# A two-layer hybrid decoder step: streamed operands moved to 16 bytes past 32, the opening splits taken by turns, the shared bias chain given priority, and the retention's old states loaded into two large slots

## The chip, the cores and the metric

The kernel runs on one core of one Trainium2 chip. The metric is device time in microseconds of one execution, lower is better. TensorE is called PE below (PEld is its loading of weights), VectorE DVE, ScalarE ACT, GpSimd POOL and SyncE SP.

## The reference

A step of a two-layer decoder on 256 prompt tokens and 8 decode tokens, all float32. Each layer runs three mixers on the same input, merges them through gates, and ends in two residual norms and a feed-forward block:

```python
u = x @ w_in                       # 1024 -> 8464 columns
q_r, k_r, v_r, g_r, z, xbc, dt_raw, q_c, k_c, v_c, gates = split(u)
o_r, s_ret_new = _retention(rotary(q_r), rotary(k_r) * RET_DK ** -0.5, v_r, s_ret)
br_a = (head_norm(o_r) * silu(g_r)) @ w_br_ret
xs, bm, cm = split(silu(causal_conv(xbc, s_conv)))
y, s_ssm_new = _ssd(xs, softplus(dt_raw + dt_bias), -exp(a_log), bm, cm, s_ssm)
br_b = group_rms((y + d_skip * xs) * silu(z)) @ w_br_ssd
o_c = sliding_window_attention(q_c, k_c, v_c, kbuf, vbuf, sinks, rel_bias)
br_c = o_c @ w_br_swa
g_a, g_b, g_c = split(sigmoid(gates), 3)
x = layer_norm(ALPHA * x + (g_a * br_a + g_b * br_b + g_c * br_c) @ w_out)
x = layer_norm(ALPHA * x + (silu(x @ w_ffn_gate) * (x @ w_ffn_up)) @ w_ffn_down)
```

The decode tokens need old states: `state_ret` (8 sequences x 4 heads x 128 x 128 per layer), `state_ssm`, convolution rows and key/value caches. All new states are outputs.

## The kernel before

**Activations are stored as [128 features, 264 tokens]**: 256 prompt tokens and 8 decode tokens side by side. A weight block of 128x128 is PE's stationary operand and a 264-column activation tile is streamed past it. To keep float32 accuracy from the fast float32r mode, every operand is split into a high and a low part. ACT writes the high part (`wh`, `xh`), DVE subtracts to get the low part (`wl`, `xl`), and `mm3` runs three matmuls per block: `wh` with `xh`, `wh` with `xl`, `wl` with `xh`. A product over 1024 features is a `gemm` of eight blocks k = 0..7, 24 matmuls into one PSUM bank.

**Where the streamed tiles lie.** The layer input is one tile for each part, `x{h,l}` of [128, 8, T + 2] with T = 264, so block k starts k * 1064 bytes behind a tile that starts at a multiple of 32. The blocks k = 0..7 start 0, 8, 16, 24, 0, 8, 16, 24 bytes past a multiple of 32. The other streamed float32r tiles are slots of 8 * T columns (`T8`: `chl`, `rhl`, `yhl`, `mh`, `ml`) or of T columns (`fh`, `fl`, the feed-forward hidden tiles). 264 columns are 1056 bytes, 33 times 32, so all of their blocks start at a multiple of 32.

**The stages of a layer.** `mixers` runs in this order: products for keys and values, queries, retention values, queries and keys, B and C of the state-space mixer (SSD), gates, and its inputs (all appear as `ps_u`); then the branches, each with gate products (`ps_gate`) and a branch product (`ps_br`); then the output product (`ps_o`). `ffn` follows with gate and up products (`ps_fg`, `ps_fu`) and the down product (`ps_fd`). `ps_z` are products on an input that is not normalized yet, with two more columns.

**What runs between.** Attention (`swa`), retention (`ret`), the SSD decay and body (`ssd_decay`, `ssd`) and state updates are generators in a queue; `pump` takes a step of one after each product. A scheduler that simulates the program then sets the final order on every engine, from the order of the code, priorities (`high_priority`) and explicit edges (`issue_after`). Each engine works through its own list in order, so whatever stands at the head of a list and waits holds up what is behind it.

**Names that the change touches.** `load_x` loads and transposes the input (`ps_x`, 24 transposes) and splits it with `xsplit`; before it, 16 matmuls on constants (`ps_warm`) run. `halves` makes the first six products of layer 0 (key/value and queries). `bias_table` builds attention's position bias: `ps_rb`, a row in DRAM, then two tables `bias`. `ret` needs old retention states in `rs0` (shown as `rs`): 512 KB per head, in a pool of two slots `SI`; head h + 1 is asked for when head h is used. 32 matmuls `ps_rso` per layer read them. `ssd` loads its old states into the same two `SI` slots (`s`). `T8` has three slots in turn: attention's result `chl`, its two tables of scores `lg`, later `rhl`, `xdt`, `yhl` and others. `on` (normalized retention output) is transposed into `ps_rt`.

Of the kernel before, what the change touches and what calls it, by code (L numbers as in the profile page):

```python
# [10 lines left out]
F32 = mybir.dt.float32  # L11
F32R = mybir.dt.float32r
AF = mybir.ActivationFunctionType
ALU = mybir.AluOpType
# [6 lines left out]
SEQ = 256  # L21
NS = 8
T = SEQ + NS
KB = D // 128
N_IN = 8464
D_FF = 2816
KF = D_FF // 128
# [5 lines left out]

WARM = 16
CONV = 1536

QR, KR, VR, GR, ZZ, XBC, DT, QC, KC, GATE = 0, 512, 1024, 1536, 2048, 3072, 4608, 4624, 5136, 5392
# [10 lines left out]
def _constants():  # L48

    secs = {}  # L50
# [12 lines left out]
    c0 = (i[None, :] >= p[:, None]).astype(np.float64)  # L63
    secs["mask"] = np.concatenate([c0, c0[:, :128]], 1)
    lg = np.log(1.0 - 2.0 ** (-5.0 - np.arange(4)))
# [41 lines left out]
class Kern:  # L107
# [88 lines left out]
    def wsplit(self, raw, shape, into=None):  # L196

        n = int(np.prod(shape))
        if into is None:
            pool = self.hps[self.nsplit % len(self.hps)]  # L200
            self.nsplit += 1
            into = tuple(pool.tile([128, 1024], F32R, tag=t, bufs=3 if pool is self.hp else 1, name=t) for t in ("wh", "wl"))
        h, l = into
        spec = {2: "p (a b) -> p a b", 3: "p (a b c) -> p a b c"}[len(shape)]
        kw = dict(zip("abc", shape))
        kw.pop("abc"[len(shape) - 1])
        hv, lv = h[:, :n].rearrange(spec, **kw), l[:, :n].rearrange(spec, **kw)
        hf = h[:, :n].bitcast(F32).rearrange(spec, **kw)
        with self.tc.high_priority(200):
            self.act(hv, raw)  # L210
            self.sub(lv, raw, hf)
# [27 lines left out]
    def load_x(self):  # L239
        nc, a, cp = self.nc, self.a, self.cp  # L240
        keep = _OFF["onehot"][0]
        self.cst = cp.tile([128, keep], F32, name="cst")
        nc.sync.dma_start(self.cst[:, 0:256], a["cst"][:, 0:256])

        self.xb = [self.xp.tile([128, KB, T + 2], F32R, name=f"x{c}") for c in "hl"]
        self.xw = [tuple(t[:, k] for t in self.xb) for k in range(KB)]
        self.x = [(h[:, :T], lo[:, :T]) for h, lo in self.xw]
        xt = [self.T4("xt")[:, :D] for _ in range(2)]
        xs = self.T4("xts")[:NS, :D]
        nc.sync.dma_start(xt[0], a["x_prompt"][0, 0:128])  # L250
        nc.sync.dma_start(xt[1], a["x_prompt"][0, 128:256])
        nc.sync.dma_start(xs, a["x_sample"][:, 0])
        self.neg = cp.tile([128, 128], F32R, name="neg")
        nc.vector.memset(self.neg.bitcast(F32), -1.0 / 128)
        self.par = [None] * DEPTH
        ps = self.pg("ps_warm")
# [3 lines left out]
        next(bias)  # L260
        self.queue.append(bias)
        for k in range(KB):
# [55 lines left out]
    def bias_table(self):  # L318
# [10 lines left out]
        self.ld(row[:, 383:385], a["sinks"].rearrange("l h -> h l"))  # L329
        yield  # L330
        ps = self.pm("ps_rb")
        self.mm(ps[:8, :129], rb, oh)
# [5 lines left out]
        for h in range(2):  # L338
            self.ld(self.bias[h], once[4 * h : 4 * h + 4].unsqueeze(1).to_broadcast([4, 128, 383]))
        yield  # L340

# [191 lines left out]
    def T8(self, name, dt=F32):  # L533
        return self.slot("t8", 8 * T, 3, name, dt)

# [24 lines left out]
    def mixers(self, l):  # L560
# [10 lines left out]
        def halves(c0, n, name, pieces, shape):  # L571

            pss = [self.pg("ps_u") for _ in range(n)]
            for i in range(2):
                raw = self.strip([(0, 128, self.win(l, c0, n * 128)[:, 4 * i : 4 * i + 4])], (4, n * 128), name)
                for u in range(0, n, 2):
# [256 lines left out]
    def ssd_decay(self, l, dtf):  # L833
# [35 lines left out]
        ps = self.pm("ps_cs")  # L869
        self.mm(ps[:, 0:32], self.c("mask")[:, :128], da[:, :32])  # L870
        self.mm(ps[:, 32:64], self.c("ones"), da[:, :32])
# [35 lines left out]
    def ssd(self, l):  # L907
# [45 lines left out]
        for g in range(2):  # L953
            ps = self.pm("ps_cb")
            self.mm(ps[:, 0:256], B(g)[:, 0:128], C(g)[:, 0:256])
            self.mm(ps[:, 256:384], B(g)[:, 128:256], C(g)[:, 128:256])
            self.mul(cbm[:, g * 384 : (g + 1) * 384], ps[:, :384], self.c("mask"))
        yield
# [38 lines left out]
        def load_state(b):  # L997
            s0, bb = self.SI("s0")[:, :1024], self.T1("cb")[:, :256]
            self.ld(
                s0.rearrange("p (m n) -> p m n", m=8),  # L1000
                a["state_ssm"][l, b].rearrange("(m two) p n -> (two p) m n", two=2),
            )
            self.ld(bb, scb[b, 256:512].partition_broadcast(128))
            loaded.append((s0, bb))
# [287 lines left out]
    def ret(self, l):  # L1292
# [34 lines left out]
        yield  # L1327
        loaded = []

        def load_state(h):  # L1330
            s0 = self.SI("rs0")[:, :1024]
            with self.tc.issue_after(self.kv_ld):
                self.ld(s0.rearrange("p (b v) -> p b v", b=8), a["state_ret"][l][:, h].rearrange("b k v -> k b v"))
            loaded.append(s0)

        load_state(0)
        po = [self.pm("ps_ro0"), self.pm("ps_ro1")]
# [19 lines left out]
        for h in range(4):  # L1357
            s0 = loaded.pop(0)
            if h < 3:
                load_state(h + 1)  # L1360
            for b in range(NS):
# [60 lines left out]
        pr, pr3 = self.gg, gg3  # L1422
        for h in range(4):
            ps = self.pm("ps_rt")
            for c in range(2):
                self.tr(ps[:, c * 128 : (c + 1) * 128], on[:, (c * 4 + h) * 128 : (c * 4 + h + 1) * 128])
            self.mul(pr3[:, h, :SEQ], ps[:, :SEQ], gg3[:, h, :SEQ])
        self.mul(pr3[:, :, SEQ:T], col(os), gg3[:, :, SEQ:T])
# [261 lines left out]
```

## Time and profile before

| | |
|---|---|
| three runs, us | 1081.92, 1082.34 (median), 1082.53 |
| the profiled execution, us | 1083.31 |
| its span, first to last instruction, us | 1081.5 |
| mean granted PE clock | 0.997 |
| PE / PEld busy | 98% / 95% |
| DVE / ACT / POOL busy | 78% / 61% / 15% |
| DMA, mean over the span | 213 GB/s |

The profiled execution lies 1.81 us above its span and 0.97 us above the median of the runs. A busy share is an average over stages; the length of one stage is read from start times within it. A matmul's duration in the profile is longer than its step to the next one, because matmuls overlap in the array: what a matmul costs is the distance between two starts.

### The profile page before, as it was taken

The page shows a single profiled execution, that of the slowest core. Times are in us where ns is not written, and L with a number is a line of the kernel's source. Part 1 is how long each engine was busy: PE and PEld are TensorE (multiplying, and loading weights), DVE is VectorE, ACT ScalarE, POOL GpSimd, SP SyncE. Part 2 cuts the span into 40 slices and gives each one's busy share as a digit, 9 for nine tenths or more (in the row PEclk, how much of TensorE's full clock was granted, in tenths as well). Part 3 has the DMA queues.
Part 4 walks back from the last instruction along what each step waited for, and adds up shares of the span by engine and source line. Part 5 has one row for each costly group of instructions (what it writes and reads, how often), then busy time and mean ns, then how long its engine had stood idle before and what let it go on. Part 6 is the DMA issues. An engine that isn't in the chain of part 4 may idle for free.

```text
span 1081.5 us, 22166 instructions
## 1 busy us (share of the span) xinstructions
PE 1064.2 (98%) x8603; PEld 1023.7 (95%) x8603; DVE 839.3 (78%) x1908; ACT 658.5 (61%) x1330; POOL 163.8 (15%) x248
## 2 busy tenths in 40 slices
PE   9999999999999999999999999999999999999998
PEld 8998998999999999999999899899899999999996
DVE  4687875898769987868699878488886899877654
ACT  4485545676656776665477755466674558666442
POOL 4200012421001012121110001053100000212300
PEclk9999999999999999999999999999999999999999
DMA  9954654994546589898774345679755546989951
GB/s 313 314 174 143 170 158 152 253 274 158 170 152 202 191 282 286 285 323 298 211 242 145 118 158 139 183 195 301 232 168 186 165 155 206 295 287 299 317 188 42
DMA packets 176826, 230.74 MB, mean 213 GB/s; under 512 B 8040, under 2 KB 151984, under 8 KB 176544
## 3 DMA queue, kind: packets, MB, share of 16 engines
q1 hardware_dynamic: 156384, 166.95, 48.3%
q0 software_dynamic: 20272, 62.34, 19.3%
q8 instruction: 68, 1.11, 0.4%
q14 instruction: 38, 0.31, 0.1%
q10 hardware_dynamic: 64, 0.03, 0.0%
HBM read 213.52 MB, written 19.61 MB: 216 GB/s over the span
## 4 chain that ended last, share of the span: by engine, by line
PE 80%; issue 12%; DVE 3%; DMA 2%; ACT 2%; POOL 1%; ACTq 0%; POOLq 0%; DVEq 0%
PE ps_u L125 13%; PE ps_fd L125 12%; PE ps_gate L125 11%; PE ps_fg L125 9%; PE ps_fu L125 9%; PE ps_br L125 8%; PE ps_z L125 5%; PE ps_o L125 5%; DMA rs<-in_state_ret_dram 1%; PE ps_y L125 1%; ACT wh L141 1%; DVE wl L146 1%; PE ps_var L125 1%; DMA csb<-scr_cs 1%; PE ps_st L125 1%
## 5 line engine op out<-in xcount | busy, mean ns | idle before, releaser
L125 PE MATMUL ps_u<-xh,wh 128*128 128x264 f32 x608 | 174.4, 289 | 2.8 <-ACT wh L141 2.6
L125 PE MATMUL ps_u<-xl,wh 128*128 128x264 f32 x608 | 173.3, 287 | 0.0
L125 PE MATMUL ps_u<-xh,wl 128*128 128x264 f32 x608 | 173.2, 288 | 0.0
L125 PEld LDWEIGHTS ps_u<-xh,wh 128*128 128x128 f32 x608 | 114.2, 189 | 6.5 <-ACT wh L141 4.5
L125 PEld LDWEIGHTS ps_u<-xh,wl 128*128 128x128 f32 x608 | 114.5, 189 | 2.3 <-issue 2.0
L125 PEld LDWEIGHTS ps_u<-xl,wh 128*128 128x128 f32 x608 | 114.4, 188 | 1.0 <-issue 0.5
L125 PE MATMUL ps_gate<-xh,wh 128*128 128x264 f32 x384 | 110.6, 291 | 0.6 <-ACT th L141 0.6
L125 PE MATMUL ps_gate<-xl,wh 128*128 128x264 f32 x384 | 110.1, 290 | 0.0
L125 PE MATMUL ps_gate<-xh,wl 128*128 128x264 f32 x384 | 109.8, 290 | 0.0
L125 PE MATMUL ps_fd<-fh,wl 128*128 128x264 f32 x352 | 100.4, 285 | 0.0
L125 PE MATMUL ps_fd<-fh,wh 128*128 128x264 f32 x352 | 100.3, 285 | 0.0
L125 PE MATMUL ps_fd<-fl,wh 128*128 128x264 f32 x352 | 99.9, 284 | 0.0
L169 POOL DMA_DIRECT2D s<-in_state_ssm_dram x32 | 28.9, 902 | 357.9 <-ACT sn L141 228.1
L146 DVE TENSOR_TENSOR wl<-w_fd,wh 128x1024 fp32r<-128x1024 f32 (+1 forms) x48 | 54.2, 1135 | 37.0 <-ACT wh L141 36.7
L125 PE MATMUL ps_fg<-xh,wh 128*128 128x264 f32 x288 | 82.0, 285 | 0.6 <-DVE v L158 0.6
L125 PE MATMUL ps_fg<-xl,wh 128*128 128x264 f32 x288 | 82.4, 286 | 0.0
L125 PE MATMUL ps_fu<-xh,wh 128*128 128x264 f32 x288 | 82.4, 286 | 0.0
L125 PE MATMUL ps_fu<-xl,wh 128*128 128x264 f32 x288 | 82.1, 285 | 0.0
L141 ACT ACTIVATE wh<-w_gate 128x1024 fp32r<-128x1024 f32 x48 | 50.6, 1057 | 51.6 <-PE ps_br L125 21.2
L125 PE MATMUL ps_fg<-xh,wl 128*128 128x264 f32 x288 | 81.8, 284 | 0.0
L125 PE MATMUL ps_fu<-xh,wl 128*128 128x264 f32 x288 | 81.8, 284 | 0.0
L141 ACT ACTIVATE wh<-w_fd 128x1024 fp32r<-128x1024 f32 (+1 forms) x48 | 47.1, 986 | 55.9 <-PE ps_fd L125 44.9
(459 smaller groups left out, 3408.2 us busy)
## 6 DMA issues: line engine op xcount, KB each, us to landing
w_gate<-in_w_in_dram SPq DMA_DIRECT2D x24, 1024.0 KB, 5.4
w_fg<-in_w_ffn_gate_dram SPq DMA_DIRECT2D x22, 1024.0 KB, 5.6
w_fu<-in_w_ffn_up_dram SPq DMA_DIRECT2D x22, 1024.0 KB, 6.2
s<-in_state_ssm_dram POOLq DMA_DIRECT2D x32, 512.0 KB, 7.2
w_fd<-in_w_ffn_down_dram SPq DMA_DIRECT2D x16, 1024.0 KB, 7.7
out_dram<-sn POOLq DMA_DIRECT2D x24, 512.0 KB, 7.6
w_qk<-in_w_in_dram SPq DMA_DIRECT2D x8, 1024.0 KB, 5.1
w_xs<-in_w_in_dram SPq DMA_DIRECT2D x8, 1024.0 KB, 5.0
```

What stands on the lines that cost most here:

```text
L125: return self.nc.tensor.matmul(out, lhsT, rhs, start=start, stop=stop).ins
L141: i = self.nc.scalar.activation(out=out, in_=in_, func=func, scale=scale, **kw)
L146: return self.nc.vector.tensor_tensor(out=out, in0=a, in1=b, op=op).ins
L169: return self.nc.gpsimd.dma_start(out, in_).ins
```

## The change

- **Addresses.** The input tiles get rows of T + 8 columns (1088 bytes, 34 times 32) and start 4 elements further in, so all eight blocks start 16 bytes past a multiple of 32. `T8` slots and the `fh`, `fl` tiles get 8 more columns, and their float32r views start 4 elements in. The weights stay at multiples of 32.
- **The start.** Four warm matmuls fewer. Only the identity (128 columns) is loaded ahead of the input; `ones` is a memset, and `mask` is stored without its third block. The decode tokens are loaded before the prompt. All transposes are issued first, blocks 4 and 5 into another PSUM pool; splits of x are taken two or four at a time between the splits of the first weights (`split_turned`).
- **Bias chain.** The second step of `bias_table` runs with priority 600.
- **Retention.** All four heads' old states are asked for at once, two heads to a `T8` slot, after the key cache's load; SSD's state loads come after the last of them. Two heads share one `ps_rt` bank and one multiplication.
- **Mask.** The product of B and C is masked on its two triangular blocks alone by DVE; ACT copies the full block.

```diff
-WARM = 16
+WARM = 12
+OFF, XP = 4, T + 8
-        nc.sync.dma_start(self.cst[:, 0:256], a["cst"][:, 0:256])
-        self.xb = [self.xp.tile([128, KB, T + 2], F32R, name=f"x{c}") for c in "hl"]
+        nc.sync.dma_start(self.cst[:, 0:128], a["cst"][:, 0:128])
+        xr = [self.xp.tile([128, KB * XP + 8], F32R, name=f"x{c}") for c in "hl"]
+        self.xb = [t[:, OFF : OFF + KB * XP].rearrange("p (k t) -> p k t", k=KB)[:, :, : T + 2] for t in xr]
+        nc.sync.dma_start(xs, a["x_sample"][:, 0])
         nc.sync.dma_start(xt[0], a["x_prompt"][0, 0:128])
         nc.sync.dma_start(xt[1], a["x_prompt"][0, 128:256])
-        nc.sync.dma_start(xs, a["x_sample"][:, 0])
+        nc.vector.memset(self.c("ones"), 1.0)
...
-            ps = self.pm("ps_x")
+            ps = (self.pg if k in (4, 5) else self.pm)("ps_x")
-            with self.tc.high_priority(400):
-                i = self.xsplit(*self.x[k], ps[:, :T])
+            self.turned.append((k, ps))
             if k == 1:
-                first = i
-        self.after = first
+                self.after = self.split_turned(2, ())
+    def split_turned(self, n, after):
+        with ExitStack() as es:
+            es.enter_context(self.tc.high_priority(400))
+            for j in after:
+                es.enter_context(self.tc.issue_after(j))
+            for k, ps in self.turned[:n]:
+                i = self.xsplit(*self.x[k], ps[:, :T])
+        del self.turned[:n]
+        return i
...
     def T8(self, name, dt=F32):
-        return self.slot("t8", 8 * T, 3, name, dt)
+        t = self.slot("t8", 8 * T + 8, 3, name, dt)
+        return t[:, : 8 * T] if dt == F32 else t[:, OFF : OFF + 8 * T]
...
+                        self.after = self.split_turned(4 if i else 2, self.split)
...
+            self.act(cbm[:, o + 128 : o + 256], ps[:, 128:256])
...
+            with self.tc.issue_after(self.old_ld):
+                self.ld(
...
-        load_state(0)
+        olds = []
+        for h in range(0, 4, 2):
+            s2 = self.T8("rs0")
+            for i in range(2):
+                s0 = s2[:, i * 1024 : (i + 1) * 1024]
+                with self.tc.issue_after(self.kv_ld):
+                    j = self.ld(s0.rearrange("p (b v) -> p b v", b=8), a["state_ret"][l][:, h + i].rearrange("b k v -> k b v"))
+                olds.append(s0)
+        self.old_ld = j
...
-            self.mul(pr3[:, h, :SEQ], ps[:, :SEQ], gg3[:, h, :SEQ])
+            self.mul(pr3[:, h : h + 2, :SEQ], ps.rearrange("p (h n) -> p h n", h=2), gg3[:, h : h + 2, :SEQ])
...
-        hh = [self.fp.tile([128, T], F32R, name=f"fh{l}_{f}") for f in range(KF)]
-        hl = [self.fp.tile([128, T], F32R, name=f"fl{l}_{f}") for f in range(KF)]
+        hh, hl = (
+            [self.fp.tile([128, T + 8], F32R, name=f"f{c}{l}_{f}")[:, OFF : OFF + T] for f in range(KF)] for c in "hl"
+        )
```

ACT's list at the start of the program, before the change (`xh` is a split of the input, `wh` one of weights):

```order
L141 ACTIVATE alh<-cst 128x128
L141 ACTIVATE xh<-ps_x 128x264 x4
L141 ACTIVATE wh<-w_kv 128x512 x2
L141 ACTIVATE xh<-ps_x 128x264
L141 ACTIVATE wh<-w_kv 128x512 x2
L141 ACTIVATE xh<-ps_x 128x264 x2
L141 ACTIVATE wh<-w_qc 128x512 x4
L141 ACTIVATE xh<-ps_x 128x264
```

The same place after it:

```order
L143 ACTIVATE alh<-cst 128x128
L143 ACTIVATE xh<-ps_x 128x264 x2
L143 ACTIVATE wh<-w_kv 128x512 x2
L143 ACTIVATE xh<-ps_x 128x264 x2
L143 ACTIVATE wh<-w_kv 128x512 x2
L143 ACTIVATE xh<-ps_x 128x264 x4
L143 ACTIVATE wh<-w_qc 128x512 x4
```

The first split of weights has moved from behind four splits of the input to behind two, and the last split of the input from behind the first query weights to ahead of them.

POOL's list in layer 0 from the key cache on, before (each is a DMA; `rs_` are retention's old states, `s_` SSD's):

```order
L169 DMA kcache<-in_cache_swa_k_dram 128x8x128
L169 DMA rs_1664<-in_state_ret_dram 128x8x128
L169 DMA rs_1875<-in_state_ret_dram 128x8x128
L169 DMA vcache<-in_cache_swa_v_dram 128x8x128
L169 DMA scr_cs<-cst_t 32x128
L1353 MEMSET qpadr 128x1024
L169 DMA scr_v<-vs 8x512
L165 DMA out_dram<-rst 128x4x128
L169 DMA rs_1925<-in_state_ret_dram 128x8x128
L169 DMA rs_1969<-in_state_ret_dram 128x8x128
L169 DMA s_2424<-in_state_ssm_dram 128x8x128
L169 DMA s_2485<-in_state_ssm_dram 128x8x128
```

And after:

```order
L171 DMA kcache<-in_cache_swa_k_dram 128x8x128
L171 DMA vcache<-in_cache_swa_v_dram 128x8x128
L171 DMA rs_1661<-in_state_ret_dram 128x8x128 x2
L171 DMA rs_1664<-in_state_ret_dram 128x8x128 x2
L171 DMA s_2417<-in_state_ssm_dram 128x8x128
L171 DMA s_2478<-in_state_ssm_dram 128x8x128
L171 DMA scr_cs<-cst_t 32x128
L1377 MEMSET qpadr 128x1024
L171 DMA scr_v<-vs 8x512
L167 DMA out_dram<-rst 128x4x128
```

Heads 2 and 3, which stood behind the outputs of retention, and SSD's first two states now stand ahead of the SSD decay's scratch row; heads 0 and 1 have moved behind the value cache.

PE's list at the old states of layer 1, before (`ps_ro` is the prompt's retention output, `ps_qkv` and `ps_rso` the decode tokens'; "..." stands for gate and branch products):

```order
L125 MATMUL ps_rsc<-qk 128x128
L125 MATMUL ps_rso<-rs_8532,qpadr 32x128 x8
L125 MATMUL ps_rso<-rs_8743,qpadr 32x128 x8
L125 MATMUL ps_gate<-xl,wh 128x264
...
L125 MATMUL ps_ro_8534<-vtok,rsc 128x128
L125 MATMUL ps_ro_8535<-vtok,rsc 128x128 x2
L125 MATMUL ps_qkv<-osq,cst 128x32
...
L125 MATMUL ps_rso<-rs_8793,qpadr 32x128 x8
...
L125 MATMUL ps_rso<-rs_8837,qpadr 32x128 x8
```

And after:

```order
L127 MATMUL ps_rsc<-qk 128x128
L127 MATMUL ps_rso<-rs_8525,qpadr 32x128 x16
L127 MATMUL ps_rso<-rs_8528,qpadr 32x128 x8
L127 MATMUL ps_ro_8531<-vtok,rsc 128x128
L127 MATMUL ps_ro_8532<-vtok,rsc 128x128 x2
L127 MATMUL ps_rso<-rs_8528,qpadr 32x128 x8
L127 MATMUL ps_qkv<-osq,cst 128x32
L127 MATMUL ps_gate<-xl,wh 128x264
```

The sixteen matmuls on heads 2 and 3, which stood between gate and branch products further down, now follow directly on those of heads 0 and 1.

## Rows read from the trace of the kernel before

**Rows 1.** The page's head: span, busy time and share of engines.

```profile
span 1081.5 us, 22166 instructions
PE 1064.2 (98%) x8603; PEld 1023.7 (95%) x8603; DVE 839.3 (78%) x1908; ACT 658.5 (61%) x1330; POOL 163.8 (15%) x248
```

**Rows 2.** Critical chain in time, layer 0's feed-forward: start us, us, what, count.

```profile
378.15 2.95 PE ps_fg L125 x24
...
469.09 2.95 PE ps_fu L125 x24
472.04 29.54 PE ps_fd L125 x243
```

**Rows 3.** Timeline of PE: block starts in one up product; the last step.

```profile
404.40 0.29 PE L125 MATMUL ps_fu<-xh,wh 128*128 128x264 f32 x1
...
405.14 0.28 PE L125 MATMUL ps_fu<-xh,wh 128*128 128x264 f32 x1
...
405.50 0.28 PE L125 MATMUL ps_fu<-xh,wh 128*128 128x264 f32 x1
...
406.60 0.28 PE L125 MATMUL ps_fu<-xh,wh 128*128 128x264 f32 x1
...
406.95 0.29 PE L125 MATMUL ps_fu<-xh,wh 128*128 128x264 f32 x1
...
407.33 0.29 PE L125 MATMUL ps_fg<-xh,wh 128*128 128x264 f32 x1
...
1069.68 0.29 PE L125 MATMUL ps_fd<-fh,wl 128*128 128x264 f32 x1
```

**Rows 4.** Timeline of all engines at the start of the program.

```profile
8.55 1.24 ACT L141 ACTIVATE xh<-ps_x 128x264 fp32r<-128x264 f32 x4 [5.32 <-PE ps_x L129]
8.98 1.45 DVE L146 TENSOR_TENSOR xl<-ps_x,xh 128x264 fp32r<-128x264 f32 x4 [5.42 <-ACT xh L141]
...
9.73 1.15 ACT L141 ACTIVATE wh<-w_kv 128x512 fp32r<-128x512 f32 x2
...
11.04 0.39 PE L125 MATMUL ps_u<-xh,wh 128*128 128x264 f32 x1
...
13.61 2.32 ACT L141 ACTIVATE wh<-w_qc 128x512 fp32r<-128x512 f32 x4 [0.85 <-DMA w_qc<-in_w_in_dram]
```

**Rows 5.** Waits of PE: line, whom for; us in total, times, longest.

```profile
PE ps_rso L125 <- DMA rs<-in_state_ret_dram: 3.0, 3, 2.1
PE ps_u L125 <- ACT wh L141: 2.6, 4, 0.8
PE ps_rt L129 <- ACT on L141: 1.3, 2, 1.0
```

**Rows 6.** Timeline of POOL and PE, layer 1: score transposes, state loads, their use.

```profile
604.44 1.04 PE L129 MATMUL ps_pT<-cst,lg 128*128 128x128 f32 x8
...
674.95 1.81 POOL L169 DMA_DIRECT2D rs<-in_state_ret_dram  x2 [7.62 <-PE ps_rso L125]
...
683.36 0.65 PE L125 MATMUL ps_rso<-rs,qpadr 128*32 128x128 f32 x16 [2.08 <-DMA rs<-in_state_ret_dram]
...
685.08 0.88 PE L125 MATMUL ps_rso<-rs,qpadr 128*32 128x128 f32 x16 [0.50 <-DMA rs<-in_state_ret_dram]
```

**Rows 7.** Busy time (x instructions) of PE, PEld, DVE, ACT, POOL; PEclk; DMA share, GB/s.

```profile
172.00:176.70 4.70, 3.19 (x16) 1.88 (x16) 2.25 (x5) 4.70 (x13) 0.00 (x0) 1.00 0.00 0
176.80:180.20 3.40, 3.40 (x18) 3.40 (x17) 1.44 (x2) 0.81 (x2) 0.00 (x0) 0.50 0.86 302
...
681.00:685.30 4.30, 1.72 (x30) 1.09 (x32) 1.22 (x1) 0.67 (x2) 0.89 (x1) 1.00 0.78 223
685.40:688.70 3.30, 3.30 (x25) 2.92 (x18) 0.43 (x1) 0.28 (x1) 0.88 (x1) 0.50 1.09 344
```

**Rows 8.** Critical chain in time, around the two stretches at half clock.

```profile
175.85 3.97 PE ps_gate L125 x20
...
685.96 4.16 PE ps_br L125 x22
```

More of the change, by code (lines that the diff above doesn't have):

```diff
@@ L63, in _constants @@
     c0 = (i[None, :] >= p[:, None]).astype(np.float64)
-    secs["mask"] = np.concatenate([c0, c0[:, :128]], 1)
+    secs["mask"] = c0[:, :128]
     lg = np.log(1.0 - 2.0 ** (-5.0 - np.arange(4)))
@@ L209, in wsplit @@
         with self.tc.high_priority(200):
-            self.act(hv, raw)
-            self.sub(lv, raw, hf)
+            i = self.act(hv, raw)
+            self.split = i, self.tt(lv, raw, hf, ALU.subtract)
         if len(shape) == 3:
@@ L261, in load_x @@
         self.queue.append(bias)
+        self.turned = []
         for k in range(KB):
@@ L330, in bias_table @@
         yield
+        urgent = ExitStack()
+        urgent.enter_context(self.tc.high_priority(600))
         ps = self.pm("ps_rb")
@@ L339, in bias_table @@
             self.ld(self.bias[h], once[4 * h : 4 * h + 4].unsqueeze(1).to_broadcast([4, 128, 383]))
+        urgent.close()
         yield
@@ L869, in ssd_decay @@
         ps = self.pm("ps_cs")
-        self.mm(ps[:, 0:32], self.c("mask")[:, :128], da[:, :32])
+        self.mm(ps[:, 0:32], self.c("mask"), da[:, :32])
         self.mm(ps[:, 32:64], self.c("ones"), da[:, :32])
@@ L956, in ssd @@
             self.mm(ps[:, 256:384], B(g)[:, 128:256], C(g)[:, 128:256])
-            self.mul(cbm[:, g * 384 : (g + 1) * 384], ps[:, :384], self.c("mask"))
+            o = g * 384
+            blk = lambda x: x.rearrange("p (b j) -> p b j", b=3)[:, 0:3:2]
+            self.mul(
+                blk(cbm[:, o : o + 384]), blk(ps[:, :384]), self.c("mask").unsqueeze(1).to_broadcast([128, 2, 128])
+            )
+            self.act(cbm[:, o + 128 : o + 256], ps[:, 128:256])
         yield
@@ L998, in load_state @@
             s0, bb = self.SI("s0")[:, :1024], self.T1("cb")[:, :256]
[L999 to L1002, printed above, removed]
+            with self.tc.issue_after(self.old_ld):
+                self.ld(
+                    s0.rearrange("p (m n) -> p m n", m=8),
+                    a["state_ssm"][l, b].rearrange("(m two) p n -> (two p) m n", two=2),
+                )
             self.ld(bb, scb[b, 256:512].partition_broadcast(128))
@@ L1327, in ret @@
         yield
[L1328 to L1334, printed above, removed]
-        load_state(0)
+        olds = []
[7 more added lines that the diff above has]
+        self.old_ld = j
         po = [self.pm("ps_ro0"), self.pm("ps_ro1")]
@@ L1357, in ret @@
         for h in range(4):
-            s0 = loaded.pop(0)
-            if h < 3:
-                load_state(h + 1)
+            s0 = olds[h]
             for b in range(NS):
@@ L1422, in ret @@
         pr, pr3 = self.gg, gg3
-        for h in range(4):
+        for h in range(0, 4, 2):
             ps = self.pm("ps_rt")
-            for c in range(2):
-                self.tr(ps[:, c * 128 : (c + 1) * 128], on[:, (c * 4 + h) * 128 : (c * 4 + h + 1) * 128])
-            self.mul(pr3[:, h, :SEQ], ps[:, :SEQ], gg3[:, h, :SEQ])
+            for i in range(2):
+                for c in range(2):
+                    o = (c * 4 + h + i) * 128
+                    self.tr(ps[:, (2 * i + c) * 128 : (2 * i + c + 1) * 128], on[:, o : o + 128])
+            self.mul(pr3[:, h : h + 2, :SEQ], ps.rearrange("p (h n) -> p h n", h=2), gg3[:, h : h + 2, :SEQ])
         self.mul(pr3[:, :, SEQ:T], col(os), gg3[:, :, SEQ:T])
@@ L1503, in ffn @@
         wu = a["w_ffn_up"][l].rearrange("(k p) c -> p k c", p=128)
-        hh = [self.fp.tile([128, T], F32R, name=f"fh{l}_{f}") for f in range(KF)]
-        hl = [self.fp.tile([128, T], F32R, name=f"fl{l}_{f}") for f in range(KF)]
+        hh, hl = (
+            [self.fp.tile([128, T + 8], F32R, name=f"f{c}{l}_{f}")[:, OFF : OFF + T] for f in range(KF)] for c in "hl"
+        )
         self.queue.append(self.updates(l))
```

## The prediction

> **What bounds the kernel.** I read the page's head first. PE is busy for 98% of the span, DVE for 78%, ACT for 61% [rows 1]: PE is the engine that ends last, and time can only come from shorter steps between its matmuls, or from the few places where it stands. The waits of PE are short: 3.0 us for retention's old states, 2.6 for splits of weights, 1.3 for `on` [rows 5]. So next I read the length of a step, from the chain in order of time. In layer 0's feed-forward, 32 gate and up products follow each other from 378.15 to 472.04 us: 93.89 us for 768 matmuls, 122.25 ns each. The down product behind them takes 29.54 us for 243, 121.56 ns each [rows 2]. Both run without a wait at full clock on the same 264 columns; what differs in their operands is where the streamed tile begins, by turns 0, 8, 16, 24 bytes past 32 in the first, always 0 in the second.
>
> The timeline of one up product shows the turns. Blocks k = 0 and 1 together take 0.74 us, block 2 (16 past) 0.36, blocks 3 to 5 1.10, block 6 (16 past again) 0.35, block 7 (24 past) 0.38 [rows 3]. Starts are rounded to 10 ns, so one block says little; I took every step of the timeline between two such matmuls of 264 columns that follow each other without a wait (under 160 ns), 6,676 of them between the first `ps_u` at 11.04 [rows 4] and the last `ps_fd` at 1069.68 [rows 3], and sorted them by the streamed tile's start. Means: 121.76 ns at 0 (3,245 steps), 123.03 at 8 (1,149), 120.52 at 16 (1,153), 123.60 at 24 (1,129).
>
> **The change part by part.**
>
> *Addresses.* 5,315 of the streamed matmuls read `x` tiles, about 1,329 in each of the four classes, and 2,208 read the other tiles, all at 0. If every one costs what the 16 class costs now, the classes give (1,329 + 2,208) x 1.24 ns = 4.4 us, 1,329 x 2.51 = 3.3 us and 1,329 x 3.08 = 4.1 us, 11.8 us in all. 568 of them are `ps_z` with 266 columns, whose own class means differ less (123.0 at 16 against 123.5 to 124.2), which takes off 0.6. I take 11 us. The trace doesn't show a product in which all blocks are at 16, and a step might depend on its neighbour's address too. Lower bound: 16 is no better than 0 in a product of equal blocks. The x tiles then go from 122.25 to about 121.7, and nothing else moves: 1,329 x (1.27 + 1.84 - 1.24) = 2.5 us. Upper bound: the class reaches what it has in the 216 steps of `ps_fg`, 119.4 ns: 5,315 x 2.85 + 2,208 x 2.16 = 20 us.
>
> [...]
>
> *The start.* The first product starts at 11.04 us. ACT had begun with four splits of the input at 8.55 (1.24 us, 0.31 each) and reached the first weights at 9.73 [rows 4]. Now two input splits stand ahead of them: 8.55 + 0.62 + 0.58 (half of 1.15) = 9.75, if the weights have landed by 9.17; rows show only that they had by 9.73. So the first matmul comes between 9.8 and 10.4, 0.6 to 1.2 us earlier. Behind it DVE (0.36 us for an input split, 0.64 for a weight's) has about 1 us of work for each 1.5 us of PE, and the query weights, landed at 13.61, are needed only after 48 steps. Earlier loads (64 KB less of constants ahead) may add some tenths. I take 1.0 us; from 0, if ACT waits for the second half of the key weights, to 1.8.
>
> *Retention's old states.* Heads 2 and 3 are asked for at 674.95, when PE releases the slots, and PE waits 2.08 and 0.50 us for them in layer 1 [rows 6]; 3.0 us with layer 0 [rows 5]. In the new order they wait only for a score slot, whose last readers are transposes ending at 605.48 [rows 6]. POOL issues four loads at 0.9 us; the old loads took from 674.95 to 685.08 at most, 10.1 us. They land by about 620, against a first use near 672. Gain 3.0 us, bounds 0 and 3.7 (with the branch products between them, which no longer break up). What is next behind that wait, `ps_qkv` and retention's norm, has PE's products beside it.
>
> *Clock.* [...] Together 2.0, bounds 0 and 3.0.
>
> *Transposes of the retention output.* PE waited 1.3 us for `on` [rows 5]. Two banks instead of four, so two releases fewer, but the same ACT work ahead: 0.5 us, bounds -0.5 and 1.3.
>
> *At nothing.* The warm matmuls run while PE waits for the input anyway; their cost would be a lower clock at 11 us if four fewer were too few, about 1.5 us as in rows 8. The bias chain moves DMAs and one DVE copy ahead of DVE work which PE doesn't wait for. The mask moves a third of four DVE instructions to ACT, under 0.4 us each beside gate products. In the open any of these would be under 0.5 us.
>
> *New waits.* The scheduler has laid out layer 0's mixers anew on every engine, and PE's list there has other products around each small matmul. The largest waits of that kind before are 0.8 and 1.0 us [rows 5]; I put one such, 1.0 us, against the change, bounds 0 and 5 (five of them).
>
> Sum: 11 + 1.0 + 3.0 + 2.0 + 0.5 - 1.0 = 16.5 us. The profiled execution took 1083.31 us (span 1081.5 and 1.81 around it), so 1066.8; it lies 0.97 us above the median of the runs, so 1065.8 in their measure.
>
> **The rivals.**
>
> *16 is as good as 0, no better.* [...] For it: the middle step of a block at 16, with the streamed operands before and after it at 16 too, is 121.6 ns, about the same as in the down product [rows 2]. Against it: the first and third steps of the same blocks, at 120.2 and 119.6. [...] Chance 0.25.
>
> *The whole class reaches the feed-forward's best.* 20 us, and 25.5 in all: 1056.8. For it: blocks 2 and 6 in rows 3; against it, `ps_gate` and `ps_u`, where the class lies at 120.5 to 121. Chance 0.12.
>
> *The waits are moved, not removed.* Steps get shorter by 11 us, but DVE and ACT (78% and 61% busy) don't get faster, so PE waits for splits and for `on` elsewhere, and 5.5 us becomes 1: 1070.3. Chance 0.10.
>
> *The change doesn't do what it says.* Step lengths follow from the order of loads and matmuls, and the classes are an accident of their places in a product; steps stay at 122, and waits return as others. Within 2 us of 1082.3. The equal count of each class in all products and its repetition in both layers speak against it. Chance 0.05.
>
> *Slower: PE's list stands at the 32 old-state matmuls.* They now stand nearly in one piece, and PE takes nothing from behind them. If the slots came free only with the attention branch's last reading of `chl` (branch products still run at 690, [rows 6, 8]), the loads would land 10 us later, 28 us after their turn near 672: slower by 10 to 40 us. It decides from the point where both layers' waits exceed 19 us. Against it: the slots are those of `lg`, free at 605. Chance 0.04.
>
> **How the numbers follow.** The forecast has 0.44. 1065.8 us, its own range 1061 to 1071. The range for 8 in 10 reaches from the best case to beyond the first rival, 1057 to 1076; outside remain no change, slower, and half of the best case. About 0.2% (2.2 us) is what a measurement of this kernel can tell. Faster holds the forecast and the first three rivals, 0.91; same 0.05; slower 0.04.
>
> **What would show it.** In the chain, a gate or up product of 24 takes 2.88 to 2.90 us instead of 2.93, the down product's 243 steps 29.3 instead of 29.54, and classes vanish within a product. If a down product stays at 29.5, the first rival holds. The first `ps_u` starts at 9.8 to 10.4. No `ps_rso` wait on a DMA is left, and PE has at most one stretch at 0.50. Wrong I would be by new PE waits of over 5 us in layer 0's mixers.

## The result, and the profile after

The changed kernel takes 1069.53 us, the median of six runs (1066.27 to 1076.00), against 1082.28 for the kernel before beside it: 0.9884 of its time, 95% interval 0.9856 to 0.9913, so 12.5 us faster (9.4 to 15.6). 1065.8 was forecast, with a range of 1057 to 1076. The direction and the size hold; the parts do not hold one by one, and that is what the experiments are about. The profiled execution took 1069.14 us.

The page's head answers to [rows 1]: PE has 8.7 us less busy time in a span that is 14.2 us shorter, so 5.5 us, more than a third, are idle time that is gone.

```profile
span 1067.3 us, 22173 instructions
PE 1055.5 (99%) x8599; PEld 1017.2 (95%) x8599; DVE 838.9 (79%) x1905; ACT 660.0 (62%) x1334; POOL 163.3 (15%) x248
```

The chain in order of time (start us, us, what), in layer 0's feed-forward, answers to [rows 2]:

```profile
408.48 2.91 PE ps_fg L127 x24
411.38 2.91 PE ps_fu L127 x24
...
466.61 29.68 PE ps_fd L127 x243
```

A gate or up product takes 2.91 us where it took 2.92 to 2.95; I had named 2.88 to 2.90, a larger fall. The down product, whose tiles moved from 0 to 16 past 32, did not come down to 29.3 but rose from 29.54 to 29.68. The waits of PE (line, whom for; us in total, times, longest) answer to [rows 5]:

```profile
PE ps_x L131 <- DMA xt<-in_x_prompt_dram: 1.3, 2, 0.8
...
PE ps_u L127 <- ACT wh L143: 0.7, 1, 0.7
...
PE ps_u L127 <- DVE wl L148: 0.6, 1, 0.6
PE ps_rt L131 <- ACT on L143: 0.4, 1, 0.4
```

No wait for `rs` is left. The timeline of POOL and PE in layer 1 shows why, against [rows 6]: the last two old heads are asked for at 600.49 instead of 674.95, 67 us before their first use.

```profile
590.71 1.83 POOL L171 DMA_DIRECT2D rs<-in_state_ret_dram  x2 [19.99 <-ACT wh L143]
600.49 1.76 POOL L171 DMA_DIRECT2D rs<-in_state_ret_dram  x2 [7.95 <-ACT wh L143]
...
668.03 1.52 PE L127 MATMUL ps_rso<-rs,qpadr 128*32 128x128 f32 x48
```

Of the windows of [rows 7] (busy us of PE, PEld, DVE, ACT, POOL; PEclk; DMA share, GB/s), the first two again, and one at the start:

```profile
11.20:14.70 3.50, 3.50 (x15) 3.02 (x16) 3.43 (x8) 3.48 (x10) 2.02 (x6) 0.51 1.06 381
...
172.00:176.70 4.70, 4.46 (x33) 3.58 (x34) 3.71 (x5) 4.70 (x14) 0.30 (x1) 1.00 0.04 3
176.80:180.20 3.40, 3.40 (x27) 3.29 (x27) 2.30 (x6) 2.85 (x6) 3.40 (x8) 1.00 0.91 317
```

Both old stretches at half clock are gone, and a new one stands at 11 us.

**Where the 14.6 us between the last matmuls of the two traces (1076.14 and 1061.50) come from.** I took the starts of all of PE's matmuls. In the trace before, a step of 264 columns takes 122 ns in the median, and 220 ns in the stretches at 0.50. My allowance for a step is 12 ns and, for 264 columns, 110 ns (half of 220), for other widths in proportion. A step that is more than 40 ns longer than this counts, by what it is longer, as standing (half-clock stretches left out); half of each half-clock stretch before the last matmul counts as lost to the clock; the rest is the steps themselves. Before: 86.9 us standing, 3.4 clock. After: 78.4 and 1.7. So 8.5 us are standing, 1.7 the clock, and 4.4 the steps. The same sum for the other kernels but off0 and off2, us, the standing by stretch (the remaining 10.6 are alike in all of them):

| | to key and value products' end | to first `ps_gate` | layer 0 to first `ps_o` | layer 1 to first `ps_gate` | layer 1 to first `ps_o` | last down product | all | clock |
|---|---|---|---|---|---|---|---|---|
| before | 6.0 | 13.5 | 18.7 | 12.3 | 19.5 | 6.3 | 86.9 | 3.4 |
| changed | 6.0 | 11.4 | 17.8 | 12.4 | 14.1 | 6.1 | 78.4 | 1.7 |
| addr | 5.2 | 14.3 | 18.1 | 12.4 | 18.1 | 6.9 | 85.6 | 5.1 |
| ret | 5.9 | 13.5 | 17.5 | 10.1 | 17.2 | 5.7 | 80.6 | 1.7 |
| addret | 5.6 | 14.2 | 17.4 | 10.2 | 17.2 | 9.3 | 84.6 | 1.7 |
| start | 6.2 | 11.2 | 25.0 | 12.3 | 17.9 | 5.5 | 88.7 | 8.5 |
| rt | 5.3 | 13.5 | 21.7 | 12.3 | 18.7 | 6.0 | 88.1 | 0.0 |
| nostart | 6.3 | 14.3 | 15.2 | 12.4 | 13.2 | 5.7 | 77.7 | 1.7 |
| nort | 6.1 | 11.4 | 17.6 | 12.4 | 14.4 | 5.2 | 77.7 | 5.1 |
| w16 | 6.0 | 14.5 | 13.6 | 12.4 | 15.0 | 6.1 | 78.2 | 0.0 |
| x16 | 6.0 | 11.4 | 17.8 | 12.4 | 13.3 | 9.5 | 80.8 | 3.4 |
| w16x16 | 5.8 | 14.5 | 13.6 | 12.4 | 13.3 | 5.2 | 75.2 | 1.7 |

### The profile page after: what moved, and what is told of

It is laid out like the page before. It is cut to its first block, busy times and chain, and to the rows that moved or that the text cites. A ratio compares the mean times of both kernels' runs of the same rounds, so it can differ in the third digit from the quotient of the medians.

```text
span 1067.3 us, 22173 instructions
## 1 busy us (share of the span) xinstructions
PE 1055.5 (99%) x8599; PEld 1017.2 (95%) x8599; DVE 838.9 (79%) x1905; ACT 660.0 (62%) x1334; POOL 163.3 (15%) x248
## 4 chain that ended last, share of the span: by engine, by line
PE 85%; issue 5%; DVE 4%; DMA 3%; ACT 2%; POOL 0%; POOLq 0%; SPq 0%; DVEq 0%; ACTq 0%
PE ps_u L127 20%; PE ps_gate L127 12%; PE ps_fg L127 9%; PE ps_fu L127 9%; PE ps_br L127 8%; PE ps_z L127 6%; PE ps_fd L127 5%; PE ps_o L127 5%; DMA w_fd<-in_w_ffn_down_dram 2%; DVE wl L148 1%; PE ps_y L127 1%; DMA s<-in_state_ssm_dram 1%; ACT wh L143 1%; DVE xl L160 1%; PE ps_var L127 1%
## 5 line engine op out<-in xcount | busy, mean ns | idle before, releaser
L143 ACT ACTIVATE wh<-w_gate 128x1024 fp32r<-128x1024 f32 x48 | 50.7, 1058 | 41.3 <-PE ps_br L127 19.5
## 6 DMA issues: line engine op xcount, KB each, us to landing
w_fd<-in_w_ffn_down_dram SPq DMA_DIRECT2D x16, 1024.0 KB, 10.6
```

Source lines behind the costliest of these rows:

```text
L143: i = self.nc.scalar.activation(out=out, in_=in_, func=func, scale=scale, **kw)
```

## The experiments

Times against the kernel before on the same chip:

| kernel | median us (runs) | ratio, 95% interval |
|---|---|---|
| off0: all streamed tiles at 0 past 32 | 1071.65 (6) | 0.9895, 0.9872 to 0.9918 |
| off2: all at 8 past 32 | 1085.82 (12) | 1.0037, 1.0019 to 1.0055 |
| x16: x at 16, the others at 0 | 1070.78 (6) | 0.9890, 0.9856 to 0.9923 |
| addr: before + addresses | 1077.79 (12) | 0.9961, 0.9942 to 0.9980 |
| ret: before + old states | 1077.00 (12) | 0.9954, 0.9935 to 0.9972 |
| addret: before + both | 1073.44 (6) | 0.9913, 0.9890 to 0.9937 |
| start: before + start | 1088.70 (12) | 1.0062, 1.0040 to 1.0084 |
| rt: before + transposes by two heads | 1086.15 (12) | 1.0038, 1.0014 to 1.0061 |
| nostart: changed without the start | 1070.54 (6) | 0.9893, 0.9868 to 0.9917 |
| nort: changed without the transposes | 1070.18 (6) | 0.9881, 0.9859 to 0.9903 |
| w16: changed, 16 warm matmuls | 1068.91 (6) | 0.9871, 0.9839 to 0.9904 |
| w16x16: w16 and x16 | 1065.38 (5) | 0.9856, 0.9829 to 0.9882 |

### Which address is it

The changed kernel lays its streamed tiles out with one constant, and with another one the order of instructions on every engine is the same. `off0` sets it to 0 (below), `off2` to 2, which is 8 bytes, `x16` keeps it for x alone, and `addr` puts the addresses into the kernel before.

```diff
-OFF, XP = 4, T + 8
+OFF, XP = 0, T + 8
```

> The changed kernel with every streamed tile at 0 past 32 bytes instead of 16; the order of instructions on every engine is the same. Theory A, 16 is the best class: ps_fg, ps_fu, ps_u steps rise from 121.2 to 121.8 or more and ps_fd stays or rises too; some 7,500 matmuls by 0.5 ns, about 4 us slower than the changed kernel (1073). Theory B, only starts at 8 and 24 cost and 0 is as good as 16: x steps 121.2 within 0.3, ps_fd back from 122.09 to 121.6, time 1069.5 within 1 us, or up to 1 us faster. Theory C, neither class matters and only that all blocks start alike: here as in theory B, but the same at 8 past 32 too.

> The changed kernel with every streamed tile at 8 past 32 bytes instead of 16; same order of instructions. Theories A and B: every step costs 1.3 to 1.9 ns more, ps_fg near 123 and ps_fd near 123.5, some 7,500 matmuls, 10 to 14 us slower than the changed kernel, about 1081. Theory C (only that all blocks start alike): steps of 121.2 and 1069.5 within 1 us.

```diff
-        return t[:, : 8 * T] if dt == F32 else t[:, OFF : OFF + 8 * T]
+        return t[:, : 8 * T]
...
-            [self.fp.tile([128, T + 8], F32R, name=f"f{c}{l}_{f}")[:, OFF : OFF + T] for f in range(KF)] for c in "hl"
+            [self.fp.tile([128, T + 8], F32R, name=f"f{c}{l}_{f}")[:, :T] for f in range(KF)] for c in "hl"
```

> The changed kernel with the x tiles at 16 past 32 as there, and the other streamed tiles (inputs of the branch, output and down products) at 0 past 32; same order of instructions on every engine. If each tile's step is set by its own start in a product of equal blocks, x steps stay at 121.2 to 121.4, ps_fd falls from 122.09 to 121.5, ps_br from 122.2 to 121.5: 2,200 steps by 0.6 ns, 1.3 us faster than the changed kernel, 1068. Rival, the down products don't follow their start but what stands before them: ps_fd at 122.1, time as the changed kernel's.

The chains of the three, one gate product and the down product of layer 0 each. off0:

```profile
397.16 2.92 PE ps_fg L127 x24
...
467.24 29.45 PE ps_fd L127 x243
```

off2:

```profile
401.54 3.00 PE ps_fg L127 x24
...
473.54 30.03 PE ps_fd L127 x243
```

x16:

```profile
396.55 2.91 PE ps_fg L127 x24
...
466.31 29.45 PE ps_fd L127 x243
```

Theory C (only likeness counts) falls: all blocks at 8 start alike and take 3.00 us, and the kernel is slower than before. It is slower than theories A and B had it, too: 1085.8 us instead of about 1081, with gate steps of 125.0 ns instead of some 123; why they are that dear was not tried. Between 0 and 16 little is left: 2.92 against 2.91 in a gate product, and the other way in the down product, 29.45 against 29.68. Sorted by tile as in the prediction, `ps_fg` steps are 121.7 ns at 0, 121.3 at 16, 125.0 at 8; `ps_fd` steps 121.5, 122.1 and 123.7. Neither theory A nor theory B holds whole. The x steps at 0 are longer than at 16, as A had it (121.8 ns over all x tiles, against 121.3), and the down product's are shorter, as B had it. Counted as above, off0's steps cost 1.7 us more than the changed kernel's, between A's 4 and B's 0, and the times (ratios 0.9895 and 0.9884) can't tell them apart. x16 has the better of each tile: `ps_fg` at 121.3 and `ps_fd` at 121.5. Its steps came as expected, its time didn't: in its profiled execution 3.4 us more standing and 1.7 us at half clock in the last down product (below) cover the 1.3.

One sign that the prediction named did not come: the classes have not vanished within a product. Taken from the starts as in the prediction, the steps of gate and up products of the changed kernel, where all blocks start at 16, are 122.2 ns in blocks 0 and 4, 119.9 in 1 and 5, 122.2 in 2 and 6, and 120.6 in 3 and 7 (some 430 steps each). In the kernel before, blocks 2 and 6, which start at 16 in both kernels, were the cheapest (120.2); now they are among the dearest. And its blocks 3 and 7, both at 24, took 122.6 and 125.1 ns. So the start past 32 is not all that sets a step, and the rival that took the classes for an accident of their places in a product has some truth. That the start counts in the mean is shown by off2, which has the changed kernel's order of instructions; what else counts was not tried.

> The kernel before with the addresses alone (every streamed tile 16 past 32; and the narrower mask, without which the wider tiles do not fit). By the prediction's term the time falls by 11 us to 1071. By the steps read in the changed kernel's trace (x products 122.3 to 121.3, ps_fd, ps_o and ps_br 0.5 ns longer) it falls by 4 us to 1078. The old-state waits (3.0 us) and the two spells at half clock stay as they were.

```diff
-        self.xb = [self.xp.tile([128, KB, T + 2], F32R, name=f"x{c}") for c in "hl"]
+        xr = [self.xp.tile([128, KB * XP + 8], F32R, name=f"x{c}") for c in "hl"]
+        self.xb = [t[:, OFF : OFF + KB * XP].rearrange("p (k t) -> p k t", k=KB)[:, :, : T + 2] for t in xr]
```

addr gains 4.2 us (2.2 to 6.3), not 11. In its profiled trace the steps give 3.4 us (its last matmul starts at 1073.10, 3.0 earlier; less 1.3 of standing, plus 1.7 more at half clock). Its steps are as long as the changed kernel's, for which the same sum gives 4.4, so such a sum is good to about 1 us. The old-state wait of layer 1 is there (1.8 us), but the stretch at half clock behind it was not, against the expectation, and a longer one stood at the start. The window of the start and that of the first old stretch:

```profile
11.00:17.80 6.80, 6.80 (x30) 6.09 (x30) 4.37 (x10) 3.11 (x8) 2.73 (x7) 0.50 1.07 359
178.20:181.60 3.40, 3.38 (x15) 3.15 (x15) 2.87 (x6) 2.23 (x6) 0.00 (x0) 0.51 0.49 157
```

### The old states

> The kernel before with the retention's old states alone moved into two of the wide slots, loaded ahead, and the SSM states' loads behind them. By the prediction's terms: the old-state waits (3.0 us) and the half-clock stretch behind them in layer 1 (1.5 us) go, 4.5 us, 1077.6 against 1082.1. Rival, waits moved and not removed: PE stands elsewhere (scores, norm, branch products) and the time is 1082 within 1 us. Rival, clock is chance: the waits' 3.0 us come, and the mean granted clock over the runs stays near the 0.996 of before; 1079.

```diff
-            s0 = loaded.pop(0)
-            if h < 3:
-                load_state(h + 1)
+            s0 = olds[h]
```

(with the loop that loads them, and the edge of the SSM loads, as in the change). ret gains 5.0 us (3.0 to 7.0), near the 4.5 of the first theory; the 3.1 of the last rival lie at the edge of the interval. Its trace has no wait for `rs` and no half-clock stretch in either layer's mixers. The mean granted clock over its 12 runs is 0.9977, over 29 runs of the kernel before beside it 0.9966: 1.2 us of the 5, which speaks for the first theory. The waits were not moved elsewhere: PE stands 2.3 us less in layer 1 from `ps_gate` to `ps_o`, 2.2 less ahead of it, where no old state is waited for, and 1.2 less in layer 0.

> The kernel before with two parts: the addresses (with the mask) and the retention's old states. If the two add, as measured alone (ratios 0.9961 and 0.9954): 9 us faster, about 1073. Rival, that the layout of layer 0's mixers, which each edit throws again, decides as much as the edits: off from 1073 by more than 3 us, with the difference in the standing of PE between the first ps_gate and the first ps_o of a layer.

The two add: 9.4 us, 1073.44. Of the changed kernel's 12.5 us these two parts hold three quarters. The rival is not needed here.

### The start, and the transposes

> The kernel before with the start alone (order of the input's loads, first splits of x and weights by turns; 16 warm matmuls, constants, bias chain as before). By the prediction 1.0 us faster, 1081, first ps_u by 10.4 us. By the changed kernel's trace, where the first ps_u came at 11.10 and the key and value products ended 1.0 us later than before: 0 to 1 us slower, first ps_u near 11.1, 1082 to 1083.

```diff
-            with self.tc.high_priority(400):
-                i = self.xsplit(*self.x[k], ps[:, :T])
-            if k == 1:
-                first = i
-        self.after = first
+            self.turned.append((k, ps))
+            if k == 1:
+                self.after = self.split_turned(2, ())
```

(with `split_turned`, its second call, and the order of the loads, as in the change). The start alone makes the kernel 6.7 us slower (4.3 to 9.1). Both times that were expected miss it; only the first `ps_u`, at 11.22, is where the second theory put it. The timeline of PE shows that PE is what it waits for, not ACT: transposes follow each other without a gap from 7.62 us to 11.22, a block of three taking 0.41 us.

```profile
7.62 0.93 PE L129 MATMUL ps_x<-cst,xt 128*128 128x128 f32 x7
8.48 0.22 PE L129 MATMUL ps_x<-cst,xts 8*128 8x8 f32 x1
...
10.70 0.44 PE L129 MATMUL ps_x<-cst,xt 128*128 128x128 f32 x2
11.07 0.22 PE L129 MATMUL ps_x<-cst,xts 8*128 8x8 f32 x1
11.22 0.39 PE L125 MATMUL ps_u<-xh,wh 128*128 128x264 f32 x1
```

The loss comes later, and most of it is the clock. The last matmul starts 7.0 us later than before; by the sum above 1.8 of them are standing and 5.1 half clock, and over the runs a mean granted clock of 0.9936 against 0.9966 makes 3.2 of the 6.7. In layer 0, 250 us behind the start, PE stands 3.77 us before a branch product until DVE has done `zt`, and is at half clock behind it (timeline; then the two windows). The other stretches at half clock are 6.8 us at 690, behind the old-state wait of layer 1, and 3.4 us at 1079.

```profile
260.97 0.81 PE L125 MATMUL ps_br<-rhl,wh 128*128 128x264 f32 x2 [3.77 <-DVE zt L158]
```

```profile
256.90:260.90 4.00, 0.30 (x6) 0.06 (x2) 4.00 (x12) 1.59 (x4) 1.13 (x3) 0.85 0.69 252
260.90:266.40 5.50, 5.43 (x24) 5.43 (x25) 4.21 (x13) 0.00 (x0) 0.00 (x0) 0.50 0.00 0
```

DVE is busy for all of 4.00 us there, with a split of weights (`wl` of `w_gate`, 1.22 us from 258.62) standing among the `xs` and `zt` that the branch needs. The prediction named "new PE waits of over 5 us in layer 0's mixers" as what would make it wrong. Here they are, 25.0 us of standing in that stretch against 18.7 before; in the changed kernel, at 17.8, they are not.

> The kernel before with the transposes of the retention's output alone, two heads to a bank. By the prediction: 0.5 us from the wait and 0.5 from the clock, 1081. Rival, the scheduler lays the rest of the layer out anew, and what it moves is worth more, either way, than the four releases: off by more than 2 us from 1082.1.

```diff
-        for h in range(4):
+        for h in range(0, 4, 2):
             ps = self.pm("ps_rt")
...
-            self.mul(pr3[:, h, :SEQ], ps[:, :SEQ], gg3[:, h, :SEQ])
+            self.mul(pr3[:, h : h + 2, :SEQ], ps.rearrange("p (h n) -> p h n", h=2), gg3[:, h : h + 2, :SEQ])
```

rt is 4.1 us slower (1.5 to 6.6): the rival. The wait that the edit aims at, for `on`, is the same as before, and new ones stand beside it (waits of PE):

```profile
PE ps_br L125 <- DVE yhl L146: 2.3, 2, 1.5
...
PE ps_u L125 <- DVE wl L146: 1.9, 1, 1.9
PE ps_rt L129 <- ACT on L141: 1.3, 2, 0.9
```

Its profiled execution (1082.01) is the fastest of its runs, so these rows show where it stands, and not all of the 4 us. What does shorten the wait for `on` is the old states' part: the same wait is 0.4 us in ret and in nort (below), which both keep one head to a bank.

```profile
PE ps_rt L129 <- ACT on L141: 0.4, 1, 0.4
...
PE ps_rt L131 <- ACT on L143: 0.4, 1, 0.4
```

> The changed kernel without the start (input loads and first splits as before; 12 warm matmuls, constants, bias chain, addresses, old states and transposes as changed). If the start is worth in this layout what it cost alone (6 to 7 us slower, by a 3.8 us wait in layer 0's branch products and the clock behind it), 1063. If its price alone was an accident of that layout, 1069.5 to 1071: the first ps_u 0.7 us later and nothing else.

> The changed kernel with the retention output's transposes one head to a bank, as before. If two heads to a bank cost by themselves (alone 5 us slower), 1065. If that was the layout's accident, 1069.5 within 2 us, or 1070 by the prediction's 0.5 us.

Both put the old lines back into the changed kernel; the diffs are those above, reversed. Neither part costs there what it costs alone: without the start the ratio is 0.9893 against 0.9884, without the transposes 0.9881, and both differences (1.0 and 0.3 us) are inside the intervals. The table of standing shows what the start does in both places where it was tried: it takes 2 to 3 us out of the stretch to the first `ps_gate` (14.3 to 11.4, and 13.5 to 11.2) and gives them back in layer 0's mixers (15.2 to 17.8, and 18.7 to 25.0). How much it gives back is a matter of the layout.

Against the expectation the first `ps_u` comes earlier without the start's order, at 10.46 in nostart, than with it, at 11.10 in the changed kernel. There ACT stands 0.80 us for the first weights, and PE, whose transposes ahead of the product end at 10.85, takes it up when ACT's second split is done at 11.06 (timeline of ACT and PE):

```profile
9.91 1.15 ACT L143 ACTIVATE wh<-w_kv 128x512 fp32r<-128x512 f32 x2 [0.80 <-DMA w_kv<-in_w_in_dram]
...
11.10 0.47 PE L127 MATMUL ps_u<-xh,wh 128*128 128x264 f32 x1
```

### The warm matmuls, and the best version

> The changed kernel with 16 warm matmuls instead of 12. Theory, the warm matmuls cover the clock: the stretch at 0.50 from 11.26 to 14.67 us of the changed kernel's trace is gone, the products of the key and value weights end about 1.5 us earlier than the 19.13 us there (near the 18.10 of before), and the time is about 1068 (1.5 us under the changed kernel's 1069.5). Rival, the clock falls because PE then waits for the input and for the split weights, whatever stood ahead: the spell at 11 us stays and the time is 1069.5 within 1 us.

```diff
-WARM = 12
+WARM = 16
```

In w16's trace the window of the start is at full clock, and the 48 steps of the key and value products are done at 18.06 instead of 19.13:

```profile
11.20:14.70 3.50, 3.50 (x26) 2.95 (x27) 3.18 (x8) 2.84 (x8) 1.83 (x6) 1.00 1.06 380
```

But one trace doesn't settle it. Of the six profiled kernels with 12 warm matmuls four have the stretch at 11 us (changed, off0, x16, nort; not off2 and nostart), of the eight with 16 one (addr; not before, ret, rt, addret, start, w16, w16x16). The traces show what PE did ahead of it: in the five that have the stretch its transposes stood for the prompt (`xt`) for 0.85 to 1.48 us, in eight of the nine others for 0 to 0.19; the ninth is nostart, which stood 0.80 and kept its clock. With 16 warm matmuls, which end at 7.32 us in the kernel before, against 5.65 for the 12 of the changed kernel, only addr stood there. So theory and rival may be one and the same: the warm matmuls cover the wait for the prompt. One trace for each kernel, and nostart among them, leave it unproven. The edit also lays layer 0 out anew: 3.1 us more standing to the first `ps_gate`, 4.2 less behind it. The time, 1068.91, lies where the theory put it and well inside the runs of the changed kernel.

> The changed kernel with 16 warm matmuls and with only the x tiles at 16 past 32 (the other streamed tiles at 0). From the two alone: steps as in that kernel (ps_fd 121.5, x 121.2), 1.3 us; and the clock's spell at 11 us gone in most executions, 1 us. 1067.5 against the changed kernel's 1069.5; faster than both kernels by the middle of the runs, but inside the spread of 1066 to 1076 that the changed kernel has. Rival: as the changed kernel within 1 us, because what spreads the runs (half-clock stretches, the last down product's weights) is not touched.

w16x16 is those two edits together: 1065.38, four of five runs within 1065.2 to 1066.5. It beats the kernel before; against the changed kernel it is 3 us lower by the ratios (0.9856 to 0.9884), and the intervals overlap.

What hid x16's gain, and may be part of what spreads the runs of these kernels, is in x16's own trace, in the last down product (waits of ACT in that stretch, then the timeline of ACT and of PE):

```profile
ACT wh L143 <- DMA w_fd<-in_w_ffn_down_dram: 5.9, 1, 5.9
```

```profile
1019.01 1.06 ACT L143 ACTIVATE wh<-w_fd 128x1024 fp32r<-128x1024 f32 x1 [5.91 <-DMA w_fd<-in_w_ffn_down_dram]
1019.97 0.41 ACT L143 ACTIVATE s<-z 128x264 f32<-128x264 f32 x1
1020.29 0.41 ACT L143 ACTIVATE sums<-z 128x264 f32<-128x264 f32 x1
1020.73 0.52 ACT L143 ACTIVATE z<-z,par 128x264 f32<-128x264 f32 x1
```

```profile
1021.29 0.44 PE L1621 MATMUL ps_y<-cst,z 128*128 128x128 f32 x2 [3.56 <-ACT z L143]
```

One split of weights waits 5.91 us for its load; the three operations on `z` stand behind it in ACT's list and begin at 1019.97, 1020.29 and 1020.73, and PE stands 3.56 us for the last of them and then runs 3.4 us at half clock (0.51 from 1021.6 to 1025.0): some 5 us. addret and off2 have the same wait of PE (3.2 and 3.0 us); the traces of the changed kernel and of w16x16 don't. Why the load is late in some of the traces was not tried.

## Why the prediction was right, and where it was not

- **Addresses** (11 us, bounds 2.5 to 20): the term that was mis-sized. 4.4 us by the steps, 4.2 by addr. What failed is "if every one costs what the 16 class costs now". The 120.5 ns of that class were measured in a mixed sequence, in blocks 2 and 6 alone; with all blocks at 16 the steps of x products take 121.3 on the mean and those same blocks 122.2 in gate and up products, and the down product rose to 122.1. The classes were no prices by the start alone: the one at 0 put x blocks of 122.2 ns together with other tiles of 121.5, and the one at 24 blocks of 122.6 and of 125.1 (gate and up products). The middle step of a block at 16, 121.6 ns, which I set down for the first rival, would have sized the term better, though what sets it is open as well. The rival "16 is as good as 0, no better" comes nearest: within 0.6 ns the two are alike. Its 2.5 us (1074.3 us with the 5.5 of the rest) are less than the 4.4 that came, because x products went to 121.3 and not to 121.7.
- **Old states** (3.0 us) and **clock** (2.0): right. ret shows 5.0 us for the two together, the wait of [rows 6] and the stretch behind it, with less standing elsewhere that I had not counted. No run shows the 2.0 us by themselves: they are my estimate that of the two windows at 0.50 in [rows 7] the one behind the old-state wait goes whole and the one behind the wait for `on` by a third. Around them 22 branch products took 4.16 us and 20 gate products 3.97 [rows 8], 1.5 us each above steps of 121.5 and 122.5 ns; the traces gave 1.7 us. In the changed trace the 1.7 us of clock are two old stretches gone and a new one at 11 us, so that near hit is in part luck. As a mean over the runs the clock alone gave less than the two stretches of [rows 8] would say: 0.995 to 0.997 before, 0.997 after, about 1 us, since the runs of both kernels have such stretches, at changing places.
- **The start** (1.0 us): wrong. The condition that I set, weights landed by 9.17, did not hold: in the changed trace ACT could begin with them only at 9.91. And I left out PE's own list: its transposes ahead of the product, which wait 1.3 us for the input, end at 10.85 there, and in start's trace, where the weights are split by 10.6, at 11.2. First `ps_u` at 11.10; what the new order saves up to the first `ps_gate` is given back in layer 0's mixers (nostart).
- **Transposes** (0.5 us): wrong in its cause. The wait fell from 1.3 us to 0.4, but by the old states' part (ret, nort); two heads to a bank leave it at 1.3 (rt), and nothing is seen in the time (nort).
- **At nothing:** the warm matmuls were given their price, 1.5 us of clock at 11 us. The changed trace pays it; that the four fewer are the cause is what the count above suggests, and is not shown. The bias chain, the constants and the mask were not run by themselves (the mask ran with addr).
- **New waits** (-1.0 us, bounds 0 and 5): the changed kernel has none: its largest wait behind the start is 0.8 us. start and rt, where one edit alone lays the mixers out anew, are 4 to 7 us slower, so the bound of 5 was not too wide.

In the profiled executions 14.6 us came where 16.5 were forecast: 4.4 by the steps for 11, 1.7 by the clock for 2.0, and 8.5 by less standing for 3.5 (3.0, 1.0 and 0.5, less 1.0). The medians differ by 12.5: about 9.4 are the two parts of addret, and some 3, with an uncertainty as large, the rest together. So the address term was too large by 7 us, and that the forecast came near all the same is luck: layer 1's mixers gave more than the waits that I had counted there. They stand 5.4 us less; the old states alone give 2.3 of that. (The 2.2 us that ret also saves ahead of them are not in the changed kernel, which stands 12.4 us there, as before.) Which of the other parts gives what is left stays open.

## What to carry to other kernels

A mean by class from a mixed sequence is no price. Sort the class once more by another mark before you use it (here by block: two blocks with the same start differed by 2.5 ns), or measure the uniform case. Where a scheduler lays out a stretch anew, an edit's value alone and its value beside the others can differ (start: 6.7 us slower alone, no difference beyond the noise in the whole), so test parts by leaving them out as well as by doing them alone. When a wait gets shorter, look whether it does so in the runs without the part that you credit (the wait for `on`). And before an earlier operand counts as an earlier product, add up the list of the engine that runs the product.

## What the runs showed of the hardware that was not expected

Streamed tiles of 264 float32r columns that begin 8 past 32 bytes cost 3% more per step in gate products when all do (3.00 us for 24, against 2.91 and 2.92 at 16 and 0) and 1 to 2% in the down product (30.03 us for 243, against 29.68 and 29.45), while in the mixed kernel the same starts looked 1% dearer than 0. Where all blocks start alike, steps still differ by 2.3 ns from block to block, with the same values four blocks on (changed kernel).

Stretches of 3.4 or 6.8 us at 0.50 of the clock stand in the traces of all kernels here but w16 and rt, before the last matmul and at changing places; the mean granted clock over the runs is 0.994 to 0.998, in w16 and rt 0.997 and 0.996. Some begin within or right behind 3.6 to 3.8 us in which PE stood (x16, start). Those at 11 us all follow a wait for the prompt: from 8 to 11 us PE was busy for 2.24 of 3.00 us both before and in addr, but from 4 to 8 us for 4.00 in the one and 3.15 in the other (windows of before, then of addr), and the clock fell behind it in addr alone. nostart stood nearly as long (0.80 us) and kept its clock, so what decides stays open.

```profile
4.00:8.00 4.00, 4.00 (x17) 3.07 (x17) 0.00 (x0) 0.00 (x0) 2.69 (x6) 1.00 0.98 317
8.00:11.00 3.00, 2.24 (x17) 1.43 (x15) 2.02 (x5) 2.45 (x7) 2.15 (x5) 1.00 1.09 364
...
4.00:8.00 4.00, 3.15 (x16) 2.39 (x16) 0.00 (x0) 0.00 (x0) 2.50 (x5) 1.00 0.95 297
8.00:11.00 3.00, 2.24 (x17) 1.44 (x15) 2.00 (x6) 2.42 (x7) 2.21 (x5) 1.00 1.10 352
```
